# A decoder layer on one core: its first product taken on the raw input, its norm multiplied in afterwards, and the last product's end in smaller pieces

## The chip, the cores and the metric

The kernel runs on one core of a Trainium2 chip. The metric is device time in microseconds (us). Three timed runs of the kernel before gave 757.86, 758.69 and 758.94, so the median is 758.69 us. Engines are named as the profile names them: PE is TensorE (PEld its weight loads), DVE is VectorE, ACT is ScalarE, POOL is GpSimd, and SP issues most of the transfers.

## The reference

A decoder layer on 512 tokens of width 1024, in fp32.

```
h = rms_norm(x, g_mix);  proj = h @ w_in
q, k, v, qi, ki, wi, conv_in, qc, gate_pre = split_cols(proj, ...)
y_att  = top-k sparse attention: index scores from qi, ki, wi choose 256 keys a row
bg, cg, u = split(conv_in);  y_conv = (bg * causal_dwconv(cg * u)) @ w_conv_out
mem_kv = rms_norm(mem, g_mem) @ w_mem_kv;  y_mem = attention of qc on the memory @ w_mem_out
merged = gates0 * y_att + gates1 * y_conv + gates2 * y_mem;  x = x + merged @ w_o
h = rms_norm(x, g_ffn);  x = x + (silu(conv(gate)) * conv(val)) @ w_down
return rms_norm(x, g_final)
```

`rms_norm(a, g)` is `a * rsqrt(mean(a*a) + 1e-6) * g` over each row.

## The kernel before

Every large product is made of three matmuls: both factors are split into a high part `hi` (a rounded copy, made by ACT) and a low part `lo` (the rest, a subtraction on DVE), and hi·hi, lo·hi and hi·lo are added in one PSUM bank. A chunk of `w_in` (512 KB) comes over SP's queue into a `raw` buffer, is split, and meets the eight 128-row chunks of the normalised input `h` in 24 matmuls with 512 columns (L150 to L152 in the trace). Most of PE's time is that.

The head, in its order:
- The memory's key and value product: the transposed memory and its weights arrive as `mkv`, 48 matmuls of 512 columns into two PSUM banks (`pkv`).
- The norm of x: four row blocks are squared on ACT with a sum (L265), POOL takes the power -1/2, the four row factors are put on diagonals (`dg`, by DVE and ACT, L312 and L315), and two matmuls with ones spread them over all partitions as `rb` (L318).
- For each of the eight chunks of x transposed (`xn`, four tiles of two chunks with the gains and 424 columns of `w_in` beside them): DVE multiplies by gain and `rb` (L345), ACT makes hi (L348), DVE lo (L351). The 424 columns are keys, values and index projections by rows; their 12 matmuls a chunk are the rows product `pn` (L354, L356, L358), 96 in all.
- The first projections of the short convolution, by channels: `cg`, `u` and `bg`, 24 matmuls each, then the same for the second third, and so on. Between them the index queries and keys are copied by ACT to the places where the score matmuls want them (`Q`, L455, sixteen copies; `K`, L444) and their low parts are moved by DMA; the score matmuls are L463.

The order on each engine is written by a scheduler at build time, except that instructions inside `keep(...)` stay in the order of the program. Eight PSUM banks are in three pools: four "at", three "mm" and one "o" (L104). A new tile of a pool waits until the one whose bank it takes was read for the last time.

The tail is `w_down`: 22 chunks stream through with eight banks open (`stream_rows`), the last three are held, and each bank is finished in turn. `after_down` adds x, squares with a sum on ACT, multiplies by g_final, takes the power on POOL, and scales both halves of the row block before it is written.

Of the kernel before, what the change touches and what calls it, by code (L numbers as in the profile page):

```python
# [17 lines left out]
P = 128  # L18
# [75 lines left out]
def layer(ctx, tc, x, mem, g_ffn, g_final, w_in, x_n, m_kv, w_cm, w_att, w_o, w_up, w_down,  # L94
# [148 lines left out]

    kv_tags = ("oath", "oatl", "ocvh", "ocvl")
    mkv, rows = [], []
    for c in range(KD // 2):
        n = 1 if c == 0 else 2
        raw = op.tile([P, 2, M + 2 * CW + 1], F32, tag=kv_tags[c], name="mkv")
        for i in range(0, 2, n):
            keep(nc.sync.dma_start(raw[:, i:i + n], m_kv[2 * c + i:2 * c + i + n].rearrange("k p c -> p k c")))  # L250
        mkv.append(raw)
        if c == 2:
            rows += [first_rows(x, b, wp, "raw", 3) for b in range(2)]
    rows += [first_rows(x, 2, wp, "raw", 3), first_rows(x, 3, op, "omeh")]
    xn = []
    for c in range(KD // 2):
        raw = ea.tile([P, 2, S + NW + 1], F32, name=f"xn{c}")
        keep(nc.sync.dma_start(raw, x_n[2 * c:2 * c + 2].rearrange("k p c -> p k c")))
        xn.append(raw)
# [14 lines left out]
    ss = ea.tile([P, 2, NB], F32, name="ss")  # L274
    pkv = [bank("o"), bank()]
    for c, raw in enumerate(mkv):
        hi = wp.tile([P, 2, 2 * CW], F32R, tag="whi", name="whi", bufs=3)
        lo = wp.tile([P, 2, 2 * CW], F32R, tag="wlo", name="wlo", bufs=3)
        for ks in ([0], [1]) if c == 0 else ([0, 1],):
# [31 lines left out]
    dg = op.tile([P, 2, NB, P], F32R, tag="ocvh", name="dg")  # L311
# [4 lines left out]
    rb = bank()  # L316
    for i in range(2):
        keep(nc.tensor.matmul(rb, ones_r, dg[:, i].rearrange("p b s -> p (b s)"), start=i == 0, stop=i == 1))  # L318

    ready = {}  # L320

    def ahead(c0):

        src = w_in[IN_STARTS.index(c0)]
        raw = wp.tile(list(src.shape), F32, tag="raw", name="raw", bufs=3)
        keep(nc.sync.dma_start(raw, src))
        hi = wp.tile(list(src.shape), F32R, tag="whi", name="whi", bufs=3)
        lo = wp.tile(list(src.shape), F32R, tag="wlo", name="wlo", bufs=3)
        keep(nc.scalar.activation(hi, raw, AF.Copy))
        keep(nc.vector.tensor_sub(lo, raw, hi.bitcast(F32)))  # L330
        ready[c0] = hi, lo


    kr = op.tile([P, MB, CW], F32, tag="oath", name="kr")
    rm = ea.tile([P, MB], F32, name="rm")
    vms = [pkv[b][:, CW:].rearrange("p (h d) -> p h d", d=HD) for b in range(MB)]
    pn = [bank("at") for b in range(NB)]
    for c, raw in enumerate(xn):
        wh = ea.tile([P, 2, NW], F32R, name=f"wnh{c}")
        wl = ea.tile([P, 2, NW], F32R, name=f"wnl{c}")  # L340
        w = raw[:, :, S:S + NW]
        for j in range(2):
            k = 2 * c + j
            xt = raw[:, j, :S]
            keep(nc.vector.scalar_tensor_tensor(xt, xt, raw[:, j, S + NW:], rb, op0=ALU.mult, op1=ALU.mult))  # L345
            if j == 0:
                keep(nc.scalar.activation(wh, w, AF.Copy))
            keep(nc.scalar.activation(h[0][:, k], xt, AF.Copy))  # L348
            if j == 0:
                keep(nc.vector.tensor_sub(wl, w, wh.bitcast(F32)))  # L350
            keep(nc.vector.tensor_sub(h[1][:, k], xt, h[0][:, k].bitcast(F32)))  # L351
            bs = [slice(b * P, (b + 1) * P) for b in range(NB)]
            for b in range(NB):
                keep(nc.tensor.matmul(pn[b][:, :NW], h[0][:, k, bs[b]], wh[:, j], start=k == 0, stop=False))  # L354
            for b in range(NB):
# [29 lines left out]
    ahead(C_U)  # L385
    for t in range(3):
# [21 lines left out]
    nc.vector.tensor_scalar_mul(bgT, bgT, 0.5)  # L408
# [340 lines left out]
    def stream_rows(w, act, kc, tail, done, sp):  # L749
# [13 lines left out]
        last = [wrows(w, k, sp) for k in range(kc - tail, kc)]  # L763
# [8 lines left out]
    h2 = (h2p.tile([P, KD, S], F32R, name="h2h"), h2p.tile([P, KD, S], F32R, name="h2l"))  # L772
# [140 lines left out]
```

## Time and profile before

| | |
|---|---|
| median of three runs | 758.69 us |
| the profiled execution | 758.13 us |
| span of its trace | 756.3 us |
| PE busy | 739.1 us, 98% of the span |
| share of PE in the chain that ended last | 95% |

The span is what the trace covers; the execution's own time is 1.83 us longer. The chain of waits is followed back from the last instruction, so its shares say which engine the end hung on. In a timeline row come the start, the duration, the engine, the line, the operation with output and inputs, and in square brackets the idle time ahead of it and what ended that.

### The profile page before, as it was taken

The page shows a single profiled execution, that of the slowest core. Times are in us where ns is not written, and L with a number is a line of the kernel's source. Part 1 is how long each engine was busy: PE and PEld are TensorE (multiplying, and loading weights), DVE is VectorE, ACT ScalarE, POOL GpSimd, SP SyncE. Part 2 cuts the span into 40 slices and gives each one's busy share as a digit, 9 for nine tenths or more (in the row PEclk, how much of TensorE's full clock was granted, in tenths as well). Part 3 has the DMA queues.
Part 4 walks back from the last instruction along what each step waited for, and adds up shares of the span by engine and source line. Part 5 has one row for each costly group of instructions (what it writes and reads, how often), then busy time and mean ns, then how long its engine had stood idle before and what let it go on. Part 6 is the DMA issues. An engine that isn't in the chain of part 4 may idle for free.

```text
span 756.3 us, 9061 instructions
## 1 busy us (share of the span) xinstructions
PE 739.1 (98%) x3428; PEld 616.7 (82%) x3428; DVE 466.8 (62%) x787; ACT 341.2 (45%) x566; POOL 17.4 (2%) x42
## 2 busy tenths in 40 slices
PE   6899999999999999999999999999999999999995
PEld 4788888888888888888899888888888888888884
DVE  4756999999777763385466565656565654121215
ACT  6658465686455543244235434343434343121214
POOL 0100002000000000000010000000000000000001
PEclk9999999999999999999999999999999999999998
DMA  9725234522122224244403232322223232323202
GB/s 340 285 95 181 84 113 125 168 66 81 56 92 74 73 74 177 92 140 140 139 29 102 94 100 96 94 101 90 105 87 109 86 110 81 114 84 111 84 28 112
DMA packets 25931, 83.37 MB, mean 110 GB/s; under 512 B 3264, under 2 KB 4416, under 8 KB 25888
## 3 DMA queue, kind: packets, MB, share of 16 engines
q1 hardware_dynamic: 25744, 82.53, 32.6%
q8 instruction: 27, 0.44, 0.2%
q10 hardware_dynamic: 144, 0.26, 0.1%
q14 instruction: 16, 0.13, 0.1%
HBM read 77.34 MB, written 2.10 MB: 105 GB/s over the span
## 4 chain that ended last, share of the span: by engine, by line
PE 95%; DMA 1%; ACT 1%; DVE 1%; issue 0%; POOL 0%; SPq 0%; POOLq 0%; ACTq 0%
PE ps_mm L151 19%; PE ps_mm L150 19%; PE ps_mm L152 19%; PE ps_at L150 9%; PE ps_at L152 9%; PE ps_at L151 9%; DMA mkv<-m_kv 1%; PE ps_at L668 1%; PE ps_o L699 1%; PE ps_at L354 1%; PE ps_at L356 1%; PE ps_at L358 1%; PE ps_at L685 1%; PE ps_o L152 1%; PE ps_o L151 1%; PE ps_o L150 1%
## 5 line engine op out<-in xcount | busy, mean ns | idle before, releaser
L161 DVE TENSOR_TENSOR wlo<-raw,whi 128x1024 fp32r<-128x1024 f32 (+2 forms) x122 | 144.7, 1187 | 193.0 <-ACT whi L160 192.9
L160 ACT ACTIVATE whi<-raw 128x1024 fp32r<-128x1024 f32 (+2 forms) x122 | 125.8, 1032 | 181.2 <-PE ps_o L152 82.3
L150 PE MATMUL ps_mm<-hhi,whi 128*128 128x512 f32 x312 | 122.4, 392 | 0.0
L151 PE MATMUL ps_mm<-hlo,whi 128*128 128x512 f32 x312 | 122.1, 391 | 0.0
L152 PE MATMUL ps_mm<-hhi,wlo 128*128 128x512 f32 x312 | 122.1, 392 | 0.0
L151 PE MATMUL ps_at<-h2l,whi 128*128 128x512 f32 (+1 forms) x216 | 78.9, 366 | 0.0
L152 PE MATMUL ps_at<-h2h,wlo 128*128 128x512 f32 (+1 forms) x216 | 78.8, 365 | 0.0
L150 PE MATMUL ps_at<-h2h,whi 128*128 128x512 f32 (+1 forms) x216 | 78.7, 366 | 0.0
L151 PEld LDWEIGHTS ps_mm<-hlo,whi 128*128 128x128 f32 x312 | 58.6, 188 | 11.6
L152 PEld LDWEIGHTS ps_mm<-hhi,wlo 128*128 128x128 f32 x312 | 58.6, 188 | 11.6
L150 PEld LDWEIGHTS ps_mm<-hhi,whi 128*128 128x128 f32 x312 | 58.6, 188 | 11.5
L150 PE MATMUL ps_mm<-h2h,whi 128*128 128x512 f32 x160 | 62.2, 389 | 0.0
L151 PE MATMUL ps_mm<-h2l,whi 128*128 128x512 f32 x160 | 62.2, 389 | 0.0
L152 PE MATMUL ps_mm<-h2h,wlo 128*128 128x512 f32 x160 | 62.2, 389 | 0.0
L151 PEld LDWEIGHTS ps_at<-h2l,whi 128*128 128x128 f32 x216 | 40.7, 189 | 6.6
L152 PEld LDWEIGHTS ps_at<-h2h,wlo 128*128 128x128 f32 x216 | 40.7, 189 | 6.5
L150 PEld LDWEIGHTS ps_at<-h2h,whi 128*128 128x128 f32 x216 | 40.6, 189 | 6.5
L151 PEld LDWEIGHTS ps_mm<-h2l,whi 128*128 128x128 f32 x160 | 30.0, 188 | 6.3
L152 PEld LDWEIGHTS ps_mm<-h2h,wlo 128*128 128x128 f32 x160 | 30.0, 188 | 6.2
L150 PEld LDWEIGHTS ps_mm<-h2h,whi 128*128 128x128 f32 x160 | 30.0, 188 | 6.2
L832 ACT ACTIVATE t<-t 128x512 f32<-128x512 f32 x22 | 13.9, 633 | 44.8 <-DVE t L514 44.7
L160 ACT ACTIVATE acth<-t 128x512 fp32r<-128x512 f32 x14 | 8.8, 632 | 40.4 <-DVE t L833 40.4
(276 smaller groups left out, 1296.0 us busy)
## 6 DMA issues: line engine op xcount, KB each, us to landing
raw<-w_up SPq DMA_DIRECT2D x44, 512.0 KB, 3.5
raw<-w_in SPq DMA_DIRECT2D x39, 512.0 KB, 3.3
raw<-w_down SPq DMA_DIRECT2D x22, 512.0 KB, 3.4
raw<-w_o SPq DMA_DIRECT2D x8, 512.0 KB, 3.5
xn<-x_n SPq DMA_DIRECT2D x4, 937.0 KB, 13.9
raw<-w_cm SPq DMA_DIRECT2D x8, 320.0 KB, 2.9
mkv<-m_kv SPq DMA_DIRECT2D x3, 769.0 KB, 8.4
rows<-x SPq DMA_DIRECT2D x4, 512.0 KB, 10.8
```

The lines of the kernel that those rows point to most:

```text
L150: nc.tensor.matmul(o, sh, mh, start=first, stop=False)
L151: nc.tensor.matmul(o, sh, ml, start=False, stop=False)
L152: nc.tensor.matmul(o, sl, mh, start=False, stop=last)
L160: nc.scalar.activation(hi, src, AF.Copy)
L161: nc.vector.tensor_sub(lo, src, hi.bitcast(F32))
L354: keep(nc.tensor.matmul(pn[b][:, :NW], h[0][:, k, bs[b]], wh[:, j], start=k == 0, stop=False))
L356: keep(nc.tensor.matmul(pn[b][:, :NW], h[0][:, k, bs[b]], wl[:, j], start=False, stop=False))
L358: keep(nc.tensor.matmul(pn[b][:, :NW], h[1][:, k, bs[b]], wh[:, j], start=False, stop=k == KD - 1))
L668: nc.tensor.matmul(pb[:, :N], QS[:, hd, b * P:(b + 1) * P], KS[i][:, g, :N], start=(i == 0), stop=(i == 1))
L685: nc.tensor.transpose(pt[:, kb * P:(kb + 1) * P], lt[:, kb * P:(kb + 1) * P], ident)
L699: nc.tensor.matmul(po[:, q0:], V[:, kb, g, :], PT[i][:, c], start=(kb == 0 and i == 0), stop=(kb == NB - 1 and i == 1))
L832: nc.scalar.activation(tt[0], tt[0], AF.Silu)
```

## The change

The rows product no longer waits for the norm of x. It takes x times the gain, split into `xh` and `xl`; its result is multiplied by the row factor `rx` where it is read out of PSUM (`rn`, V and `wiN`). The first `cg` projection also runs on these raw parts (tile `pc`), and its result is multiplied by `rb` into `cg0`. The normalised `h`, which all other projections need, is made later in pieces (`h_split`) between these steps. `rb` is now copied from PSUM to SBUF by ACT. The transfers of the head are put in another order: the memory's weights first, then x's columns and rows mixed. The squares of the memory's rows, their power and the scaled copies out of `pkv` move behind the sixteen `Q` copies, so both banks of `pkv` stay taken until then. PE starts with 15 transposes of the identity whose results nobody reads.

In the tail the last product holds four chunks instead of three, in the buffers of `h2`; the last bank's 512 columns are finished as two pieces of 256, and the product with g_final goes to a tile of its own, ahead of the sum of squares.

The diff, cut to what the text speaks of:

```diff
+    idle = bank("at")
+    for i in range(15):
+        keep(nc.tensor.transpose(idle[:, :P], ident, ident))
...
-        n = 1 if c == 0 else 2
+        n = 1 if c < 2 else 2
...
+    first_cols(0, 0, 2)
+    rows += [first_rows(x, b, wp, "raw", 3) for b in range(3)]
+    first_cols(1, 0, 1)
+    rows.append(first_rows(x, 3, op, "omeh"))
+    first_cols(1, 1, 1)
+    first_cols(2, 0, 2)
+    first_cols(3, 0, 2)
+    ready = {}
+    def early(c0):
+        src = w_in[IN_STARTS.index(c0)]
+        raw = wp.tile(list(src.shape), F32, tag="raw", name="raw", bufs=3)
+        keep(nc.sync.dma_start(raw, src))
+        ready[c0] = raw
+    early(C_CG)
+    keep(nc.sync.dma_start(ropeN, rope_n))
+    early(C_U)
     memn = [first_rows(mem, 0, op, "omel"), first_rows(mem, 1, op, "omeh")]
-    keep(nc.sync.dma_start(ropeN, rope_n))
     keep(nc.sync.dma_start(par, params))
+    early(C_BG)
...
+    pn = [bank("at") for b in range(NB)]
+    xg = [op.tile([P, 3, S], F32R, tag=t, name="xg") for t in kv_tags] + [ea.tile([P, 2, S], F32R, name=f"xg{i}") for i in range(2)]
+    xh = [xg[k // 3 * 2][:, k % 3] for k in range(KD)]
+    xl = [xg[k // 3 * 2 + 1][:, k % 3] for k in range(KD)]
+    wn = []
...
+        keep(nc.scalar.activation(wh[:, sl], w, AF.Copy))
+        for j in js:
+            keep(nc.scalar.activation(xh[2 * c + j], raw[:, j, :S], AF.Copy, scale=raw[:, j, S + NW:]))
+        keep(nc.vector.tensor_sub(wl[:, sl], w, wh[:, sl].bitcast(F32)))
+        for j in js:
+            keep(nc.vector.scalar_tensor_tensor(xl[2 * c + j], raw[:, j, :S], raw[:, j, S + NW:], xh[2 * c + j].bitcast(F32),
+                                                op0=ALU.mult, op1=ALU.subtract))
...
+    def h_split(*ks):
+        for k in ks:
+            xt = xn[k // 2][:, k % 2, :S]
+            keep(nc.vector.scalar_tensor_tensor(xt, xt, xn[k // 2][:, k % 2, S + NW:], rb, op0=ALU.mult, op1=ALU.mult))
+            keep(nc.scalar.activation(h[0][:, k], xt, AF.Copy))
+            keep(nc.vector.tensor_sub(h[1][:, k], xt, h[0][:, k].bitcast(F32)))
...
+    cols_split(0, [0, 1])
+    rows_products(0, 1)
+    for b in range(3):
+        squares(rows[b], ss[:, 0, b:b + 1])
+    cols_split(1, [0])
+    rows_products(2)
+    squares(rows[3], ss[:, 0, 3:4])
     rx = ea.tile([P, NB], F32, name="rx")
     rh = ea.tile([P, NB], F32R, name="rh")
     rl = ea.tile([P, NB], F32, name="rl")
     power(ss[:, 0], rx)
+    cols_split(1, [1])
...
+    rb, cg0 = (lambda t: (t[:, 0], t[:, 1]))(g0p.tile([P, 2, S], F32, tag="g0", name="rb"))
+    cols_split(2, [0, 1])
+    keep(nc.scalar.activation(rb, pr, AF.Copy))
+    rows_products(4, 5)
+    h_split(0)
+    cols_split(3, [0, 1])
+    rows_products(6, 7)
+    h_split(1)
     ahead(C_CG)
-    for b in range(MB):
-        keep(nc.vector.scalar_tensor_tensor(VM[:, b, :, HD:], vms[b], rm[:, b:b + 1], VM[:, b, :, 0:HD].bitcast(F32),
-                                            op0=ALU.mult, op1=ALU.subtract))
-    rn = op.tile([P, NB, NIH + 1, IDXD], F32, tag="ocvl", name="rn")
+    h_split(2, 3, 4)
+    pc = bank()
+    for k in range(KD):
+        wh, wl = (x[:, k, :] for x in ready[C_CG])
+        for i, (a, b) in enumerate(((wh, xh[k]), (wh, xl[k]), (wl, xh[k]))):
+            keep(nc.tensor.matmul(pc, a, b, start=k == 0 and i == 0, stop=k == KD - 1 and i == 2))
...
     ahead(C_U)
+    h_split(5)
+    keep(nc.vector.tensor_mul(cg0, pc, rb))
+    h_split(6, 7)
+    ahead(C_BG)
...
+    rm = const.tile([P, MB], F32, name="rm")
+    for b in range(MB):
+        squares(memn[b], ss[:, 1, b:b + 1])
+    power(ss[:, 1, :MB], rm)
...
+        keep(nc.scalar.activation(kr[:, b], pkv[b][:, :CW], AF.Copy, scale=rm[:, b:b + 1]))
+        keep(nc.scalar.activation(VM[:, b, :, 0:HD], v, AF.Copy, scale=rm[:, b:b + 1]))
...
+        if c == 0:
+            cg = cg0
+        else:
+            pc = project(C_CG + c * P)
+            cg = rp.tile([P, S], F32, tag="rr", name="rr", bufs=2)
+            nc.scalar.activation(cg, pc, AF.Copy)
...
+                fin = fine and (b, hf) == (NB - 1, 1)
+                n = 256 if fin else 512
                 for i, wt in enumerate(last):
-                    step(b, kc - tail + i, wt, hf)
-                done(b, hf * 512, hf * 512 + 512, acc[b][hf])
+                    step(b, kc - tail + i, wt, hf, 0, n)
+                done(b, hf * 512, hf * 512 + n, acc[b][hf][:, :n])
+                if fin:
+                    rest = bank("at")[:, :n]
+                    for i, wt in enumerate(last):
+                        step(b, kc - tail + i, wt, hf, n, 512, rest, kc - tail)
+                    nc.vector.tensor_add(x1[:, b, D - n:], acc[b][hf][:, n:], x1[:, b, D - n:])
+                    done(b, D - n, D, rest)
...
+        xg = fp.tile([P, 512], F32, tag="t0", name="xg", bufs=2)
+        tc.keep_in_program_order(nc.vector.tensor_mul(xg, x1[:, b, 512:], gl[:, 512:]))
+        nc.vector.tensor_add(st[:, 0:1], st[:, 0:1], s1)
...
-    stream_rows(w_down, act, NF, 3, after_down, wp)
...
+    tails = [h2p.tile([P, 4, KD, P], F32R, tag=n, name="t" + n) for n in ("h2h", "h2l")]
+    def hold(i, src):
+        raw = load(src.rearrange("p (k c) -> p k c", c=P))
+        with tc.high_priority(offset=400):
+            split(tails[0][:, i], tails[1][:, i], raw)
+        return tails[0][:, i], tails[1][:, i]
+    stream_rows(w_down, act, NF, 4, after_down, hold, fine=True)
```

The scheduler's order around the second third of the convolution, on ACT. `Q` and `K` are the index copies, `rr` the copy of a finished `cg` out of PSUM, `rs` its first tap. Before:

```order
L520 ACTIVATE rr<-ps_mm 128x512
L396 ACTIVATE rQ<-ps_at 128x384 x2
L160 ACTIVATE hvh<-rQ 128x384
L455 ACTIVATE Q_478<-rQ 32x384 x3
L394 ACTIVATE rK<-ps_at 32x512
L329 ACTIVATE whi<-raw 128x1024
L160 ACTIVATE whi<-raw 128x1024
L455 ACTIVATE Q_478<-rQ 32x384 x8
L160 ACTIVATE hvh<-rQ 128x384
L455 ACTIVATE Q_478<-rQ 32x384 x2
L444 ACTIVATE K_479<-rK 32x512
```

The same engine and place now. Ahead of these rows, from the last high part of `h` on, stand two `whi`, two `rQ`, one `rK` and a third `whi`:

```order
L160 ACTIVATE hvh<-rQ 128x384
L504 ACTIVATE Q_538<-rQ 32x384 x11
L493 ACTIVATE K_539<-rK 32x512
L504 ACTIVATE Q_538<-rQ 32x384 x4
L160 ACTIVATE hvh<-rQ 128x384
L504 ACTIVATE Q_538<-rQ 32x384
L287 ACTIVATE rows,ss<-rows 128x1024
L160 ACTIVATE whi<-raw 128x1024
L287 ACTIVATE rows,ss<-rows 128x1024
L590 ACTIVATE rs<-rb,par 128x512
L160 ACTIVATE whi<-raw 128x1024
L585 ACTIVATE rr<-ps_mm 128x512
```

The copy `rr` of the first `cg` is gone; the two squares of the memory's rows (L287) have come behind the sixteen `Q` copies, and the copy `rr` of the second `cg` out of PSUM is last.

On PE, at the end of the second `cg` projection; `ps_mm_831` before and `ps_mm_876` now is the second `u` projection, and the matmuls from K4 and Q4 are the first index scores. Before:

```order
L152 MATMUL ps_mm_789<-hhi_84,wlo_793 128x512
L150 MATMUL ps_mm_831<-hhi_84,whi_834 128x512
L151 MATMUL ps_mm_831<-hlo_85,whi_834 128x512
L152 MATMUL ps_mm_831<-hhi_84,wlo_835 128x512
L150 MATMUL ps_mm_831<-hhi_84,whi_834 128x512
L151 MATMUL ps_mm_831<-hlo_85,whi_834 128x512
L152 MATMUL ps_mm_831<-hhi_84,wlo_835 128x512
L150 MATMUL ps_mm_831<-hhi_84,whi_834 128x512
L151 MATMUL ps_mm_831<-hlo_85,whi_834 128x512
L463 MATMUL ps_at_526<-K4_479,Q4_478 128x256
```

Now:

```order
L152 MATMUL ps_mm_834<-hhi_84,wlo_838 128x512
L525 MATMUL ps_at_598<-K4_539,Q4_538 128x256
L525 MATMUL ps_at_601<-K4_539,Q4_538 128x256
L525 MATMUL ps_at_606<-K4_539,Q4_538 128x256
L525 MATMUL ps_at_611<-K4_539,Q4_538 128x256
L525 MATMUL ps_at_616<-K4_539,Q4_538 128x256
L150 MATMUL ps_mm_876<-hhi_84,whi_879 128x512
```

Five score matmuls have come ahead of the second `u` projection, where eight of its matmuls stood ahead of the first score before.

On DVE, where `h` is made; `hlo` is its low part, `xg` the low part of x times the gain, `wnl` that of the 424 columns. Before:

```order
L345 SCALAR_TENSOR_TENSOR xn_138<-xn_138,ps_mm 128x512
L351 TENSOR_TENSOR hlo<-xn_138,hhi 128x512
L345 SCALAR_TENSOR_TENSOR xn_140<-xn_140,ps_mm 128x512
L350 TENSOR_TENSOR wnl_367<-xn_140,wnh_366 128x848
L351 TENSOR_TENSOR hlo<-xn_140,hhi 128x512
L345 SCALAR_TENSOR_TENSOR xn_140<-xn_140,ps_mm 128x512
L351 TENSOR_TENSOR hlo<-xn_140,hhi 128x512
L330 TENSOR_TENSOR wlo<-raw,whi 128x1024
```

Now:

```order
L340 TENSOR_TENSOR wnl<-xn_145,wnh 128x848
L342 SCALAR_TENSOR_TENSOR xg<-xn_145,xg 128x512 x2
L360 SCALAR_TENSOR_TENSOR xn_143<-xn_143,rb 128x512
L362 TENSOR_TENSOR hlo<-xn_143,hhi 128x512
L340 TENSOR_TENSOR wnl<-xn_146,wnh 128x848
L342 SCALAR_TENSOR_TENSOR xg_269<-xn_146,xg_268 128x512 x2
L360 SCALAR_TENSOR_TENSOR xn_143<-xn_143,rb 128x512
L362 TENSOR_TENSOR hlo<-xn_143,hhi 128x512
L369 TENSOR_TENSOR wlo<-raw,whi 128x1024
L360 SCALAR_TENSOR_TENSOR xn_144<-xn_144,rb 128x512
L362 TENSOR_TENSOR hlo<-xn_144,hhi 128x512
```

When the last tile's columns are split, DVE had made six chunks of `h` and begun the seventh before, and has made one now. The second follows at once, three more behind the low part of the `cg` weights, and the last three only behind the rope of the index rows (`rn`) and the low part of the `u` weights.

## Rows read from the trace of the kernel before

**Rows 1.** The page: the chain that ended last, by engine.

```profile
PE 95%; DMA 1%; ACT 1%; DVE 1%; issue 0%; POOL 0%; SPq 0%; POOLq 0%; ACTq 0%
```

**Rows 2.** PE's waits: total us, number of times, longest.

```profile
PE ps_o L295 <- ACT mT L285: 6.0, 3, 4.8
PE ps_at L354 <- ACT hhi L348: 1.5, 1, 1.5
```

**Rows 3.** Timeline of ACT around the norm of x.

```profile
15.10 1.06 ACT L282 ACTIVATE whi<-mkv 128x1024 fp32r<-128x1024 f32 x1 [0.62 <-DMA mkv<-m_kv]
...
18.86 0.19 ACT L265 ACTIVATION_READ_ACCUMULATOR rows<-rows 128x1 f32 x1
20.95 1.28 ACT L315 ACTIVATE dg<-ident,rl 128x128 fp32r<-128x128 f32 x4 [1.91 <-DVE rl L310]
```

**Rows 4.** Windows: us, busy of PE, PEld, DVE, ACT, POOL; PEclk, DMA share, GB/s.

```profile
23.00:24.00 1.00, 0.00 (x0) 0.00 (x0) 1.00 (x2) 0.43 (x2) 0.00 (x0) 1.00 1.04 416
24.00:25.00 1.00, 0.71 (x3) 0.69 (x4) 1.00 (x2) 0.23 (x1) 0.00 (x0) 0.84 1.02 409
25.00:26.00 1.00, 1.00 (x5) 0.93 (x4) 0.78 (x2) 0.18 (x1) 0.00 (x0) 0.50 1.04 418
```

**Rows 5.** Timeline of DVE: making h, then the rope stretch.

```profile
23.48 1.03 DVE L350 TENSOR_TENSOR wnl<-xn,wnh 128x848 fp32r<-128x848 f32 x1
24.43 0.69 DVE L351 TENSOR_TENSOR hlo<-xn,hhi 128x512 fp32r<-128x512 f32 x1
25.04 0.74 DVE L345 SCALAR_TENSOR_TENSOR xn<-xn,ps_mm 128x512 f32<-128x512 f32 x1
26.48 0.69 DVE L351 TENSOR_TENSOR hlo<-xn,hhi 128x512 fp32r<-128x512 f32 x1 [0.70 <-ACT hhi L348]
27.09 0.74 DVE L345 SCALAR_TENSOR_TENSOR xn<-xn,ps_mm 128x512 f32<-128x512 f32 x1
...
44.11 0.84 DVE L376 COPY rn<-ps_at 128x288 f32<-128x288 f32 x2 [1.22 <-PE ps_at L358]
...
47.55 1.22 DVE L330 TENSOR_TENSOR wlo<-raw,whi 128x1024 fp32r<-128x1024 f32 x1
```

**Rows 6.** ACT by line, 50 to 66 us: busy us, mean ns | idle before.

```profile
L455 ACT ACTIVATE Q<-rQ 32x384 fp32r<-32x384 f32 x16 | 8.4, 522 | 0.2
L160 ACT ACTIVATE whi<-raw 128x1024 fp32r<-128x1024 f32 x2 | 2.1, 1055 | 0.0
L160 ACT ACTIVATE hvh<-rQ 128x384 fp32r<-128x384 f32 x2 | 1.1, 526 | 0.0
L396 ACT ACTIVATE rQ<-ps_at 128x384 f32<-128x384 f32 x2 | 0.9, 488 | 0.1
L444 ACT ACTIVATE K<-rK 32x512 fp32r<-32x512 f32 x1 | 0.6, 632 | 0.0
```

**Rows 7.** DMA issues, 40 to 75 us: KB each, median us to landing.

```profile
Q<-hvl SPq DMA_DIRECT2D x16, 48.0 KB, 1.9
```

**Rows 8.** Timeline of PE: rows product, then first matmuls of projections.

```profile
24.29 1.45 PE L354 MATMUL ps_at<-wnh,hhi 128*128 128x424 f32 x4 [1.50 <-ACT hhi L348]
...
28.25 0.94 PE L354 MATMUL ps_at<-wnh,hhi 128*128 128x424 f32 x4
29.03 0.94 PE L356 MATMUL ps_at<-wnl,hhi 128*128 128x424 f32 x4
...
56.56 0.39 PE L150 MATMUL ps_mm<-hhi,whi 128*128 128x512 f32 x1
...
67.44 0.39 PE L150 MATMUL ps_mm<-hhi,whi 128*128 128x512 f32 x1
```

**Rows 9.** Timeline of the tail.

```profile
748.67 0.69 DVE L844 TENSOR_TENSOR x<-ps_o,x 128x512 f32<-128x512 f32 x1
749.39 0.63 ACT L845 ACTIVATE y<-x 128x512 f32<-128x512 f32 x1 [0.25 <-DVE x L844]
...
752.10 0.40 ACTq L859 DMA_DIRECT2D out<-y  x1
```

More of the change, by code (lines that the diff above doesn't have):

```diff
@@ L251, in layer, with first_cols @@
         mkv.append(raw)
[L252 to L259, printed above, removed]
+    xn = [ea.tile([P, 2, S + NW + 1], F32, name=f"xn{c}") for c in range(KD // 2)]
+    def first_cols(c, i, n):
+        keep(nc.sync.dma_start(xn[c][:, i:i + n], x_n[2 * c + i:2 * c + i + n].rearrange("k p c -> p k c")))
+    first_cols(0, 0, 2)
[14 more added lines that the diff above has]
+    early(C_U)
     memn = [first_rows(mem, 0, op, "omel"), first_rows(mem, 1, op, "omeh")]
-    keep(nc.sync.dma_start(ropeN, rope_n))
     keep(nc.sync.dma_start(par, params))
+    early(C_BG)
     def squares(src, dst):
@@ L278, in layer @@
         lo = wp.tile([P, 2, 2 * CW], F32R, tag="wlo", name="wlo", bufs=3)
-        for ks in ([0], [1]) if c == 0 else ([0, 1],):
+        for ks in ([0], [1]) if c < 2 else ([0, 1],):
             w = raw[:, ks[0]:ks[-1] + 1, M:M + 2 * CW]
@@ new lines, in layer, with cols_split @@
+    wn = []
+    def cols_split(c, js):
+        raw = xn[c]
+        if js[0] == 0:
+            wn.append([ea.tile([P, 2, NW], F32R, tag="wn" + i, name="wn" + i, bufs=2) for i in "hl"])
+        wh, wl = wn[c]
+        sl = slice(js[0], js[-1] + 1)
+        w = raw[:, sl, S:S + NW]
+        keep(nc.scalar.activation(wh[:, sl], w, AF.Copy))
[5 more added lines that the diff above has]
+                                                op0=ALU.mult, op1=ALU.subtract))
@@ new lines, in rows_product, with rows_products @@
+    def rows_product(k, part):
+        w = wn[k // 2][part == 1][:, k % 2]
+        for b in range(NB):
+            keep(nc.tensor.matmul(pn[b][:, :NW], (xl if part == 2 else xh)[k][:, b * P:(b + 1) * P], w,
+                                  start=k == 0 and part == 0, stop=k == KD - 1 and part == 2))
+    def rows_products(*ks):
+        for k in ks:
+            for part in range(3):
+                rows_product(k, part)
+    def h_split(*ks):
+        for k in ks:
+            xt = xn[k // 2][:, k % 2, :S]
+            keep(nc.vector.scalar_tensor_tensor(xt, xt, xn[k // 2][:, k % 2, S + NW:], rb, op0=ALU.mult, op1=ALU.mult))
+            keep(nc.scalar.activation(h[0][:, k], xt, AF.Copy))
+            keep(nc.vector.tensor_sub(h[1][:, k], xt, h[0][:, k].bitcast(F32)))
@@ new lines, in ahead @@
+    def ahead(c0):
+        raw = ready[c0]
+        hi = wp.tile(list(raw.shape), F32R, tag="whi", name="whi", bufs=3)
+        lo = wp.tile(list(raw.shape), F32R, tag="wlo", name="wlo", bufs=3)
+        keep(nc.scalar.activation(hi, raw, AF.Copy))
+        keep(nc.vector.tensor_sub(lo, raw, hi.bitcast(F32)))
+        ready[c0] = hi, lo
+    cols_split(0, [0, 1])
[4 more added lines that the diff above has]
+    rows_products(2)
@@ L315, in layer @@
         keep(nc.scalar.activation(dg[:, 1, b], ident, AF.Copy, scale=rl[:, b:b + 1]))
-    rb = bank()
+    rows_product(3, 0)
+    rows_product(3, 1)
+    pr = bank()
     for i in range(2):
[L318 to L331, printed above, removed]
@@ L456, in layer @@
                 move(Q4[64 + 32 * i:96 + 32 * i, 4 * t + j, :], ql[src])
+    rm = const.tile([P, MB], F32, name="rm")
+    for b in range(MB):
+        squares(memn[b], ss[:, 1, b:b + 1])
+    power(ss[:, 1, :MB], rm)
+    kr = op.tile([P, MB, CW], F32, tag="omel", name="kr")
+    for b in range(MB):
+        v = pkv[b][:, CW:].rearrange("p (h d) -> p h d", d=HD)
+        keep(nc.scalar.activation(kr[:, b], pkv[b][:, :CW], AF.Copy, scale=rm[:, b:b + 1]))
+        keep(nc.scalar.activation(VM[:, b, :, 0:HD], v, AF.Copy, scale=rm[:, b:b + 1]))
+        keep(nc.vector.scalar_tensor_tensor(VM[:, b, :, HD:], v, rm[:, b:b + 1], VM[:, b, :, 0:HD].bitcast(F32), op0=ALU.mult,
+                                            op1=ALU.subtract))
     for b in range(1, NB):
```

95 lines of the change are left out of this document (32 added, 63 removed).

## The prediction, written before the result was known

> **What bounds the kernel now.** I read the page first: the chain that ended last is 95% PE [rows 1]. So time is won only where PE waits, and any new wait of PE is paid in full. The list of PE's waits comes next: 4.8 us at the start for the memory's first operand, 1.5 us in one piece for the first `hi` of h [rows 2], and little else. Then the windows and the timeline of the stretch around that wait: PE idles for the whole of 23 to 24 us, and for most of 24 to 26 us the granted clock is half, 0.84 and then 0.50 [rows 4]. The twelve matmuls of the first chunk of the rows product start at 24.29 and the next chunk at 28.25, 3.96 us, where later four take 29.03 - 28.25 = 0.78, so twelve 2.34 [rows 8]. The wait thus costs about 1.6 us again in clock behind it. The change goes for this place. After it PE runs without a wait: the first `bg` projection starts at 56.56 and the second `u` projection at 67.44, two projections or 48 matmuls later, 10.88 / 48 = 0.2267 us each [rows 8].
>
> **The start.** The 15 transposes stand in PE's first wait of 4.8 us [rows 2], so I put them at nothing. Were they longer than that wait they would cost up to 1 us, but they would still end ahead of the place that decides below.
>
> **The factor `rb` comes later.** The four row blocks of x are now mixed with the columns. Ahead of the end of the fourth, SP's queue has moved 6.69 MB (by the tiles' shapes, mkv 3.15, `xn0` 0.96, half of `xn1` 0.48, four row blocks 2.10); before, 4.20 MB (mkv 3.15 and two row blocks) had landed when ACT took the last mkv at 15.10 [rows 3]. At 411 GB/s, the middle of 409 to 418 [rows 4], the 2.49 MB more are 6.06 us: the last block lands at 21.2, and its square, priced as the `whi` of the same 1024 columns at 1.1 [rows 3], ends at 22.3. From the end of the squares (18.86 + 0.19 = 19.05) to the end of `dg` (20.95 + 1.28 = 22.23) it took 3.18 [rows 3]; so `dg` ends at 25.5 on ACT, against 22.2. The rows product does not wait for it, which is the gain. But `h` does, and all projections but one need `h`.
>
> **DVE then makes `h` in a queue.** A chunk takes 27.09 - 25.04 = 2.05: multiply, 0.70 of waiting for ACT's hi, subtract [rows 5]. The split of x adds work that was not there: a tile's two `xg`, priced as the multiply at 0.70 each, beside the `wnl` of 24.43 - 23.48 = 0.95 [rows 5]. Behind `dg`, ACT makes the next tile's hi (1.0). Then DVE does two blocks of `wnl`, two `xg` and one chunk, 4.4 each; the low part of the `cg` weights 1.15; three chunks 6.15; `rn` and rope, as 47.55 - 44.11 = 3.44; the low part of the `u` weights 1.15; one chunk 2.05; `cg0` 0.7; two chunks 4.1. [rows 5] That is 27.5, from 26.5 to 54.0. The last chunk's hi is 0.61 earlier (its subtract), at 53.4. With two or three matmuls behind, the first `u` ends at 54.7, 1.9 ahead of before. PE has waits in this stretch, but they lie beside DVE's queue. The low part of the `bg` weights, behind that last hi, is ready only at 53.4 + 1.0 + 1.15 = 55.6, which takes some 0.8 back: the head gains about 1.1, and the second `cg` ends at about 66.4.
>
> **ACT then has everything at once.** This is the step that decides. Before, the index copies `Q` were spread from 52 us on. Now all of them stand behind the last hi of `h`, and ahead of `rr`, which frees the PSUM bank of the second `cg`. Because `pkv` keeps its "mm" bank until after the index copies, only two such banks go round, and the second `u` projection must have the one that `rr` frees. From 53.4 ACT has: five `whi` 5.25, two `rQ` 0.9, two `hvh` 1.1, sixteen `Q` 8.4, one `K` 0.6 [rows 6]; one `rK`, the tap `rs` and `rr`, each priced as that `K` of 512 columns, 1.9; and two squares, priced as `whi`, 2.1. That is 20.2. Long instructions back to back overlap by about 0.08, as 23.48 + 1.03 against 24.43 on DVE [rows 5]; for twelve or so that is 1.0 less. So `rr` ends at 53.4 + 19.2 = 72.6, and the second `u` starts there against 67.44: 5.2 late. The five first scores are done by then; 256 columns at 0.78 / 4 x 256 / 424 = 0.12 each [rows 8] give back 0.6. The lag is 4.6. The low ends: if fewer of these instructions stand in the way, it falls to the wait for the moves (a rival below); the high end, with every instruction at its full mean and the last hi at 54.0, is 6.2.
>
> **The clock.** Between 66.4 and 72.6 PE would have five short matmuls. In the trace before, PE had two from 20 us to 24.29, and the clock fell to 0.50 for 1.6 us' worth of loss. I take 1.6 again; the bounds are 0 and twice that, 3.3, if two such stretches follow. The Trainium skill ("TensorE: Matmul & The Clock Gate", section "HAM oscillation — how this bites in real kernels") says that a wait between bursts of matmuls makes the next burst start at the low clock, and that each such wait pays anew. The fall after 23 us in this trace agrees; by the rule the sum has the 1.6, without it 0.
>
> **The tail.** From the last add at 748.67 to the output's transfer at 752.10 are 3.43 us [rows 9]. A last piece of 256 columns makes the add (0.69) and the square (0.63) shorter, by 0 to a half; I take 0.35 together. The product with g_final hides beside the square. The 24 short matmuls in place of 12 cost 24 x 0.12 - 12 x 0.2267 = 0.15. Net -0.2, between -0.7 and +0.2. The fourth held chunk moves work that PE does anyway: nothing.
>
> **Sum.** Against the profiled 758.13: lag 4.6 + clock 1.6 - tail 0.2 = +6.0, so 764.1; the median was 0.56 above the profiled run, so 764.7. The head's gain of 1.1 does not appear in it: it is swallowed by the wait for ACT.
>
> **Rivals.**
> - The clock stays up during the second wait, as five score matmuls lie in it and the waits are in several pieces. For it: they are more than the two `dg` matmuls of 20 to 24 us. Against it: the whole is longer. Then 764.7 - 1.6 = 763.1.
> - The bank is not what holds the second `u`; only the index copies and their moves do. The sixteenth `Q` ends about 4.5 ahead of `rr` (two squares, two `whi`, `rs` and `rr`, less overlap), at 67.9; its low part needs 1.9 from issue to landing [rows 7], so the last scores end at about 70.2. Lag 70.2 - 67.44 - 0.6 = 2.2: 760.7 with the clock up, 762.3 with it down. Against it: the order of PE and `rr`'s place at the very end of ACT's list.
> - Worse: DVE's queue is longer (ACT, which serves it with hi, also has V, `rn` and the weights between), so that the last hi comes at 55, or the clock falls for two stretches. 1.6 more: 766.3, up to 768.
> - Not slower: ACT keeps up and PE never waits there, as before, when ACT had the same copies and PE had none of its waits in this stretch. PE then starts the second `u` at 67.0 with the scores done, 1.04 better, and the tail gives 0.2: 757.4. It decides if `rr` ends by 67 us, 5.6 earlier than I work out; sixteen `Q` alone take 8.4 behind a chunk that cannot come before `rb`. Its ends are 756.5 and 758.7.
>
> **How the numbers follow.** The forecast 0.50, the clock stays 0.19, only the index copies 0.10, worse 0.09, not slower 0.12. This measurement tells 0.2%, 1.5 us, from no change. Half of the last case is below 757.2 and half within the bound: faster 0.06, same 0.07 (with a little from the index copies), slower 0.87. The range goes from 760.0 to 768.0: it holds the first four cases and the bounds of the lag and of the clock, and leaves out the last one.
>
> **What would show it.** In the trace after: `dg` ends near 25.5; the rows product has no wait for hi of h; the last `hlo` ends near 54; ACT is without a gap from 53 to 73; PE has a wait for the scores from 66 and then one of some 2 us for the second `u` that ends with ACT's `rr`; the granted clock falls behind it. The tail from the last add to the output's transfer is about 0.3 shorter. Wrong would be a `rr` that ends before 68, a third free bank, or a fourth row block that lands before 19 us, which would bring all later steps forward by as much.

## The result: 0.9% slower, and the profile after

The changed kernel takes 765.49 us in the median of three runs against 758.43 (ratio 1.0093, 95% interval 1.0073 to 1.0113), 7.1 us more. Forecast were 764.7 us and a range of 760.0 to 768.0. A fourth run, the profiled one, was disturbed as a whole (2792 us) and is left out of this median, and all rows here are from a second trace of the same kernel, whose four runs gave 765.72 us in the median (ratio 1.0093, interval 1.0079 to 1.0107). Its span is 764.0 us, 7.7 above that of before.

The chain that ended last, by engine, answers to [rows 1]; PE's share has fallen from 95% to 89%:

```profile
PE 89%; ACT 2%; DVE 1%; issue 1%; POOLq 0%; POOL 0%; ACTq 0%
```

PE's longer waits, in total us, number and longest, answer to [rows 2]. The wait for the first hi of h is gone, and so are most of the 6.0 us for the memory's operands, where the transposes now stand: the memory's first matmul starts at 4.82 as against 4.78. Later in the head others have come:

```profile
PE ps_at L439 <- DVE rn L427: 2.4, 1, 2.4
PE ps_mm L150 <- ACT rr L585: 2.0, 1, 2.0
PE ps_mm L150 <- ACT whi L368: 1.7, 1, 1.7
...
PE ps_at L525 <- DMA K<-kl: 1.4, 1, 1.4
PE ps_at L525 <- DMA Q<-hvl: 1.4, 2, 0.9
```

The second row and the last two, four waits, are one stretch in the timeline of PE. The last matmul of the second `cg` starts at 67.15; the five scores come in three pieces, each after a wait for a transfer; the second `u` starts at 73.95, when ACT's `rr` has freed its bank, where [rows 8] have 67.44:

```profile
67.15 0.39 PE L152 MATMUL ps_mm<-hhi,wlo 128*128 128x512 f32 x1
68.97 0.60 PE L525 MATMUL ps_at<-K,Q 128*128 128x256 f32 x3 [1.43 <-DMA K<-kl]
70.06 0.36 PE L525 MATMUL ps_at<-K,Q 128*128 128x256 f32 x1 [0.48 <-DMA Q<-hvl]
71.36 0.55 PE L525 MATMUL ps_at<-K,Q 128*128 128x256 f32 x1 [0.94 <-DMA Q<-hvl]
73.95 0.79 PE L150 MATMUL ps_mm<-hhi,whi 128*128 128x512 f32 x1 [2.04 <-ACT rr L585]
...
77.53 0.52 PE L152 MATMUL ps_mm<-hhi,wlo 128*128 128x512 f32 x1
77.89 0.39 PE L150 MATMUL ps_mm<-hhi,whi 128*128 128x512 f32 x1
```

The chain that ended last passes through `rr` into this `u`, and not through the transfers:

```profile
73.42 0.49 ACT rr L585
...
73.95 0.79 PE ps_mm L150
```

The nine matmuls from 73.95 to 77.89 take 3.94 us, at 0.2267 each they would take 2.04: 1.9 lost. The windows of this stretch and of the earlier one around the rope (columns as in [rows 4]) show why. The granted clock is at half from about 47 us, when the wait for the rope ends, to 50.5, and again from 71, while PE still waits, until 77.8.

```profile
48.00:50.00 2.00, 2.00 (x10) 1.75 (x10) 1.30 (x3) 0.63 (x1) 0.00 (x0) 0.50 0.26 49
...
71.00:72.00 1.00, 0.55 (x1) 0.29 (x1) 1.00 (x1) 1.00 (x3) 0.06 (x1) 0.50 0.38 88
...
76.00:77.00 1.00, 1.00 (x4) 0.80 (x3) 1.00 (x4) 0.97 (x3) 0.00 (x0) 0.50 0.95 344
77.00:78.00 1.00, 1.00 (x4) 0.77 (x4) 1.00 (x3) 0.00 (x0) 0.00 (x0) 0.60 0.84 221
```

The timeline of ACT: from the last hi of h at 53.92 to the end of `rr` at 73.89 it has no gap. The index copies begin at 58.94. Three `whi` stand ahead of them; behind them stand the two squares of the memory's rows, two more `whi` and the tap `rs`. The first row is the diagonals `dg`, which end at 24.61 + 1.28 = 25.89.

```profile
24.61 1.28 ACT L391 ACTIVATE dg<-ident,rl 128x128 fp32r<-128x128 f32 x4 [1.16 <-DVE rl L386]
...
53.92 0.63 ACT L361 ACTIVATE hhi<-xn 128x512 fp32r<-128x512 f32 x1 [1.43 <-DVE xn L360]
54.46 1.04 ACT L368 ACTIVATE whi<-raw 128x1024 fp32r<-128x1024 f32 x1
...
58.94 5.86 ACT L504 ACTIVATE Q<-rQ 32x384 fp32r<-32x384 f32 x11
...
68.72 1.06 ACT L287 ACTIVATE rows<-rows 128x1024 f32<-128x1024 f32 x1
...
73.32 0.57 ACT L585 ACTIVATE rr<-ps_mm 128x512 f32<-128x512 f32 x1
```

And the timeline of DVE, whose queue for h begins at 26.73 behind `dg` and ends with the last low part at 55.28:

```profile
26.73 1.04 DVE L340 TENSOR_TENSOR wnl<-xn,wnh 128x848 fp32r<-128x848 f32 x1 [1.61 <-ACT wnh L337]
...
43.24 0.94 DVE L419 TENSOR_SCALAR rn<-ps_at,rx 128x288 f32<-128x288 f32 x2
...
47.30 1.22 DVE L369 TENSOR_TENSOR wlo<-raw,whi 128x1024 fp32r<-128x1024 f32 x1
...
54.59 0.69 DVE L362 TENSOR_TENSOR hlo<-xn,hhi 128x512 fp32r<-128x512 f32 x1 [0.70 <-ACT hhi L361]
```

PE reaches the last low part of `h` before DVE has it, and begins the first `bg` at 55.90:

```profile
55.33 0.50 PE L151 MATMUL ps_mm<-hlo,whi 128*128 128x512 f32 x1 [0.23 <-DVE hlo L362]
...
55.90 0.40 PE L150 MATMUL ps_mm<-hhi,whi 128*128 128x512 f32 x1
```

### The profile page after: what moved, and what is told of

It reads as the page before. It is cut to its first block, busy times and chain, and to the rows that moved or that the text cites. A ratio compares the mean times of both kernels' runs of the same rounds, so it can differ in the third digit from the quotient of the medians.

```text
span 2790.2 us, 9151 instructions
## 1 busy us (share of the span) xinstructions
PE 2781.8 (100%) x3455; PEld 1585.2 (57%) x3455; DVE 480.9 (17%) x801; ACT 351.9 (13%) x578; POOL 16.9 (1%) x42
## 4 chain that ended last, share of the span: by engine, by line
PE 99%; issue 1%; DVE 0%; POOL 0%; ACT 0%; POOLq 0%
PE ps_mm L152 19%; PE ps_mm L150 19%; PE ps_mm L151 19%; PE ps_at L152 9%; PE ps_at L151 9%; PE ps_at L150 9%; PE ps_at L348 4%; PE ps_mm L413 1%; PE ps_o L764 1%; PE ps_at L733 1%; PE ps_at L750 1%; PE ps_o L152 1%; PE ps_o L150 1%; PE ps_o L151 1%; PE ps_at L525 1%
## 5 line engine op out<-in xcount | busy, mean ns | idle before, releaser
L150 PE MATMUL ps_mm<-hhi,whi 128*128 128x512 f32 x304 | 355.8, 1170 | 0.0
L152 PE MATMUL ps_mm<-hhi,wlo 128*128 128x512 f32 x304 | 354.8, 1167 | 0.0
L151 PE MATMUL ps_mm<-hlo,whi 128*128 128x512 f32 x304 | 354.3, 1166 | 0.0
L151 PE MATMUL ps_at<-h2l,whi 128*128 128x512 f32 (+1 forms) x216 | 217.9, 1009 | 0.0
L152 PE MATMUL ps_at<-h2h,wlo 128*128 128x512 f32 (+1 forms) x216 | 217.7, 1008 | 0.0
L150 PE MATMUL ps_at<-h2h,whi 128*128 128x512 f32 (+1 forms) x216 | 217.4, 1008 | 0.0
L152 PEld LDWEIGHTS ps_mm<-hhi,wlo 128*128 128x128 f32 x304 | 147.2, 484 | 113.3 <-issue 112.3
L152 PE MATMUL ps_mm<-h2h,wlo 128*128 128x512 f32 x160 | 176.0, 1100 | 0.0
L150 PE MATMUL ps_mm<-h2h,whi 128*128 128x512 f32 x160 | 175.9, 1099 | 0.0
L151 PE MATMUL ps_mm<-h2l,whi 128*128 128x512 f32 x160 | 175.9, 1099 | 0.0
```

The lines of the kernel that those rows point to most:

```text
L150: nc.tensor.matmul(o, sh, mh, start=first, stop=False)
L151: nc.tensor.matmul(o, sh, ml, start=False, stop=False)
L152: nc.tensor.matmul(o, sl, mh, start=False, stop=last)
```

## The experiments

Theory A is the prediction's: the second `u` waits for the bank that `rr` frees, `rr` stands at the end of ACT's long queue, and the clock falls behind the wait. The rivals: B, only the index copies and their moves hold PE; C, the head itself is late; D, part of the loss is the tail's. Every edit is against the changed kernel unless said otherwise, and every ratio is to the kernel before on the same chip: 758.43 us for the first four runs, 759.03 for "Work from the start of the wait" and "And work for PE during the rope", 758.52 for the other four. Differences from the changed kernel are from its 765.72 us.

**The same kernel again.** No edit.

> The changed kernel once more, unaltered, for a trace. Theory A (the second u projection waits for the PSUM bank that ACT's copy rr frees at the end of a long queue): 764 to 767 us; PE waits from about 66 to 72.6 us in pieces, the last of them ended by ACT's rr copy (L585), and the granted clock falls behind it. Rival B (only the index copies and their moves hold PE): the long wait ends with the first scores (L525), and the second u projection starts without a wait behind them. Rival C (the head itself is late, by the order of the transfers and DVE's queue): the first u projection ends later than 56.6 us.

Measured: 765.72 us. The rows above are its trace. The last wait ends with `rr`, as A has it. The three waits that B names are there too, 2.85 us in all, but the last of them ends 2 us ahead of `rr`. C is wrong by its own sign: the first `u` ends at 55.90, which is 0.66 ahead of before.

**The memory's squares early.**

```diff
-    h_split(2, 3, 4)
+    h_split(2)
...
+    squares(memn[0], ss[:, 1, 0:1])
+    h_split(3)
+    squares(memn[1], ss[:, 1, 1:2])
+    power(ss[:, 1, :MB], rm)
+    h_split(4)
...
     h_split(5)
+    kr = op.tile([P, MB, CW], F32, tag="omel", name="kr")
+    for b in range(MB):
...
+        keep(nc.scalar.activation(kr[:, b], pkv[b][:, :CW], AF.Copy, scale=rm[:, b:b + 1]))
+        keep(nc.scalar.activation(VM[:, b, :, 0:HD], v, AF.Copy, scale=rm[:, b:b + 1]))
...
```

What is added here has gone from behind the `Q` copies.

> The squares of the memory's rows, their power and the scaled copies out of pkv stand between the h pieces again, so that pkv's bank is free for the second u projection and ACT's queue has 2 us less behind the index copies. A: the wait of about 6 us and the slow clock behind it go, 757.5 to 760 us. B: the index copies and moves stay where they are, so most of the wait stays, 762 to 764. C: no gain, 765 or more, since these instructions lengthen the queue that makes h.

Measured: 758.86 us, ratio 1.0003 (0.9994 to 1.0012). Nearly the whole loss hangs on where six instructions of ACT stand (two squares and four copies; POOL's power and two instructions of DVE moved with them). In the windows of its trace PE is full from 66 to 70 us, at full clock:

```profile
66.00:67.00 1.00, 1.00 (x6) 0.82 (x5) 0.66 (x1) 0.96 (x3) 0.00 (x0) 1.00 0.34 77
67.00:70.00 3.00, 3.00 (x15) 2.48 (x14) 0.58 (x2) 2.90 (x6) 0.00 (x0) 1.00 0.36 82
```

A is right and C wrong as the main cause. B falls too, though this run does not part it from A cleanly: with a bank free the scheduler put the second `u` ahead of the first scores on PE, so their transfers are no longer waited for. Nor does it part the bank from the shorter queue, since it alters both; the next run does.

**The bank freed by DVE.**

```diff
-            nc.scalar.activation(cg, pc, AF.Copy)
+            if c == 1:
+                nc.vector.tensor_copy(cg, pc)
+            else:
+                nc.scalar.activation(cg, pc, AF.Copy)
```

> Only one thing is altered: the second cg is copied out of PSUM by DVE instead of ACT, so its bank is freed without ACT's queue. A: the wait ahead of the second u projection goes, that for the first scores (some 2 us) stays, 760 to 762.5 us. B: no change, 764 to 767. C: no change.

Measured: 760.36 us, ratio 1.0021 (1.0012 to 1.003), 5.4 below the changed kernel. ACT's queue is as long as before, less one copy, and PE's timeline shows which wait stayed: the one for the moved keys, 1.43 us. The clock does not fall behind it.

```profile
67.09 0.39 PE L152 MATMUL ps_mm<-hhi,wlo 128*128 128x512 f32 x1
68.91 0.61 PE L525 MATMUL ps_at<-K,Q 128*128 128x256 f32 x3 [1.43 <-DMA K<-kl]
69.35 0.46 PE L150 MATMUL ps_mm<-hhi,whi 128*128 128x512 f32 x1
```

So the copy's place costs 5.4 us of the loss, its clock included. Of what is left, 1.9 us against the kernel before, 1.43 is the wait for the moved keys. The two waits for moved queries are gone as well, because PE now has matmuls of `u` to do meanwhile.

**The tail alone**, on the head of before (the functions `stream_rows`, `after_down` and `hold` of the change).

> The head of the kernel before with the tail of the change (four held chunks, last 512 columns in two pieces, g_final beside the sum). A: 758.2 us, 0.2 less than before, between -0.7 and +0.2. Rival D (part of the loss is the tail's: 24 short matmuls, one more bank, the held chunks' splits): 759.5 or more.

Measured: 758.04 us, ratio 0.9991 (0.9982 to 1.0): 0.4 less, D is wrong. In its timeline the last add and the output's transfer are 2.63 us apart where [rows 9] have 3.43. POOL's power between them takes 0.55:

```profile
749.74 0.42 DVE L855 TENSOR_TENSOR x<-ps_at,x 128x256 f32<-128x256 f32 x1 [0.28 <-PE ps_at L152]
...
751.04 0.55 POOL L867 TENSOR_TENSOR st<-st,mhalf 128x1 f32<-128x1 f32 x1 [4.63 <-DVE st L866]
...
752.37 0.40 ACTq L873 DMA_DIRECT2D out<-y  x1
```

In the kernel before, the same power takes 0.92, with DVE's product with g_final beside it:

```profile
750.23 0.68 DVE L852 TENSOR_TENSOR x<-x,gl 128x512 f32<-128x512 f32 x1
750.39 0.92 POOL L853 TENSOR_TENSOR st<-st,mhalf 128x1 f32<-128x1 f32 x1 [2.61 <-DVE st L849]
```

**Work in the second part of the wait.**

```diff
         squares(memn[b], ss[:, 1, b:b + 1])
+        idle = bank("at")
+        for i in range((16, 8)[b]):
+            nc.tensor.transpose(idle[:, i % 4 * P:i % 4 * P + P], memn[b][:, i % 8 * P:i % 8 * P + P], ident)
```

> The changed kernel with 24 transposes of the memory's squared rows, whose results nobody reads, ahead of the first scores: 16 run when ACT has made the first square (about 70 us), 8 after the second (about 72), so PE is no longer idle for most of the wait. The second u projection still waits for rr. If the loss behind the wait is the clock (theory A's second term), the granted clock stays at full speed there and the time falls by 1.5 to 1.9 us, to 763.8 to 764.3. If the slow matmuls behind the wait have another cause, or the transposes don't hold the clock up, no change: 765 to 766.5.

Measured: 765.08 us, ratio 1.0086 (1.0072 to 1.01): no change that can be told from the changed kernel's 1.0093. That is outside what was expected if the clock is the cause (763.8 to 764.3), so by its time alone it speaks against the clock; the trace says why it does not. Before the first transpose PE was idle for 2.38 us. The clock was still full when it began, fell a us later and was back at the end of the transposes; the transposes themselves ran at half clock and, with the scores behind them, took so long that the second `u` came 1.71 us later than in the changed kernel, and then ran at full speed:

```profile
70.00:71.00 1.00, 0.77 (x7) 0.78 (x8) 0.00 (x0) 1.00 (x3) 0.00 (x0) 1.00 0.32 75
71.00:72.00 1.00, 1.00 (x7) 1.00 (x6) 0.84 (x1) 1.00 (x3) 0.00 (x0) 0.51 0.31 72
...
75.00:76.00 1.00, 0.78 (x5) 0.52 (x5) 1.00 (x3) 1.00 (x4) 0.00 (x0) 1.00 0.70 176
```

```profile
70.23 4.51 PE L513 MATMUL ps_at<-ident,rows 128*128 128x128 f32 x24 [2.38 <-ACT rows L287]
...
75.66 0.40 PE L150 MATMUL ps_mm<-hhi,whi 128*128 128x512 f32 x1
```

**Work from the start of the wait.**

```diff
-        ql = halves(r, ip, SQ)[1]
+        qh, ql = halves(r, ip, SQ)
+        if t == 1:
+            idle = bank("at")
+            for i in range(10):
+                nc.tensor.matmul(idle[:, :SQ], qh[:, :P], qh, start=True, stop=True)
...
         squares(memn[b], ss[:, 1, b:b + 1])
+        idle = bank("at")
+        for i in range(8):
+            nc.tensor.transpose(idle[:, i % 4 * P:i % 4 * P + P], memn[b][:, i * P:(i + 1) * P], ident)
```

> The wait of the changed kernel filled from nearly its beginning: ten matmuls of 384 columns on the second half of the index queries (ready at about 68.2 us), then eight transposes behind each of the two squares; nobody reads their results. The second u projection still waits for rr at about 73.5 to 74. If the clock falls because PE stood idle, it now stays at full speed through the wait, and the time falls by 1.5 to 1.9 us against the changed kernel, to 763.8 to 764.4. If these fillers don't count as work for the clock, or if the fall has another cause, the matmuls behind rr are slow again: 765 to 766.5.

Measured: 763.61 us, ratio 1.0065 (1.0052 to 1.0077), some 2.1 below the changed kernel. PE is at work again 0.66 us after the second `cg`, the windows keep the full clock, and the second `u` starts at 73.56, behind `rr` as ever, and at full speed: its first nine matmuls end at 75.73, after 2.17 us instead of 3.94:

```profile
67.81 2.03 PE L504 MATMUL ps_at<-hvh 128*128 128x384 f32 x10 [0.66 <-ACT hvh L160]
...
73.56 0.50 PE L150 MATMUL ps_mm<-hhi,whi 128*128 128x512 f32 x1
...
75.73 0.39 PE L150 MATMUL ps_mm<-hhi,whi 128*128 128x512 f32 x1
```

```profile
71.00:72.00 1.00, 0.49 (x4) 0.49 (x5) 0.68 (x1) 1.00 (x4) 0.37 (x2) 1.00 0.25 58
...
74.00:75.00 1.00, 1.00 (x6) 0.83 (x5) 1.00 (x2) 1.00 (x4) 0.00 (x0) 1.00 0.60 159
```

So the clock's part is shown: the wait alone costs what it lasts, and idling through it costs some 1.8 us more (3.94 - 2.17; the rest of the 2.1 is that the second `u` started 0.39 earlier here).

**h in an overlapped order on DVE.**

```diff
-            keep(nc.vector.tensor_sub(h[1][:, k], xt, h[0][:, k].bitcast(F32)))
...
+            if i:
+                low(ks[i - 1])
+        low(ks[-1])
...
-    h_split(5)
     keep(nc.vector.tensor_mul(cg0, pc, rb))
-    h_split(6, 7)
+    h_split(5, 6, 7)
```

(`low(k)` is the subtraction of chunk k; it now stands behind the multiplication of the next chunk. The multiplication that makes `cg0` stands ahead of the last three chunks, where it parted the first of them from the other two.)

> The changed kernel with one edit: DVE multiplies the next chunk of h before it subtracts the one before, so it does not wait 0.70 us for ACT's hi in most of the chunks. Theory A with the queue of DVE ahead of it: h is done some 3.5 us earlier, ACT's queue starts earlier by as much and rr with it: 761 to 763 us. If ACT's queue is set by something other than the last piece of h: no change, 765 to 766.5.

Measured: 762.23 us, ratio 1.0045 (1.0032 to 1.0057), 3.5 below the changed kernel. The timelines of ACT and PE show the last hi at 49.87 and the end of `rr` at 69.84, both 4.05 earlier, with the same 19.3 us between them; PE's wait has only moved:

```profile
49.87 0.63 ACT L364 ACTIVATE hhi<-xn 128x512 fp32r<-128x512 f32 x1 [0.76 <-DVE xn L363]
...
69.27 0.57 ACT L589 ACTIVATE rr<-ps_mm 128x512 f32<-128x512 f32 x1
```

```profile
66.28 0.71 PE L529 MATMUL ps_at<-K,Q 128*128 128x256 f32 x4 [1.92 <-DMA K<-kl]
...
69.90 0.80 PE L150 MATMUL ps_mm<-hhi,whi 128*128 128x512 f32 x1 [2.24 <-ACT rr L589]
```

That shows the first link of the chain: here the last hi came 4.05 us earlier, and so did the second `u`. Of the 4.05, 3.5 reach the median.

**Both edits.** The overlapped order, the memory's squares behind the fourth chunk of h, and the copies out of `pkv` straight behind the last:

```diff
+    h_split(2, 3)
...
+    squares(memn[0], ss[:, 1, 0:1])
+    squares(memn[1], ss[:, 1, 1:2])
+    power(ss[:, 1, :MB], rm)
+    h_split(4)
...
     h_split(5, 6, 7)
     ahead(C_BG)
+    kr = op.tile([P, MB, CW], F32, tag="omel", name="kr")
...
```

> Both edits together: h in the overlapped order, the memory's squares between its pieces, and the scaled copies out of pkv straight behind the last piece, so that a bank is free and no long wait is left. A: the two gains add, since one shortens what stands ahead of the index copies and the other takes the wait behind them: 754.5 to 756.5 us, faster than the kernel before. If the head is bound by something other than DVE's queue (the transfers, PE itself): 758 to 759, as with the early squares alone.

Measured: 756.46 us, ratio 0.9973 (0.9962 to 0.9984). The two gains, 3.5 and 6.9 by themselves, are 9.3 together, so they nearly add; that is the slow end of what A expected. PE's waits and a window show what is left, the wait for the rope and the slow clock behind it:

```profile
PE ps_at L455 <- DVE rn L437: 2.4, 1, 2.4
```

```profile
48.00:50.00 2.00, 2.00 (x7) 1.61 (x6) 1.96 (x4) 1.04 (x2) 0.00 (x0) 0.50 0.66 217
```

**And work for PE during the rope**, on top of both edits:

```diff
+    ahead(C_U)
     rn = ea.tile([P, NB, NIH + 1, IDXD], F32, name="rn")
...
     keep(nc.vector.tensor_add(a2, a2, rt[:, 1]))
-    ahead(C_U)
```

> As the version with both edits, and the split of the first u weights stands ahead of the rope instead of behind it, so that PE has some 13 matmuls of the first u projection to do while the rope is made, and is not idle for 2.4 us there. DVE has the same work in all, so the last piece of h comes no earlier. If the slow clock behind that wait (0.50 from 47 to 51 us) was on the path: 1 to 2 us less, 754.5 to 755.5. If h alone bounds this stretch: no change, 756 to 757.

Measured: 754.57 us, ratio 0.9946 (0.9932 to 0.9959), some 4 us faster than the kernel before and 1.9 below the version with both edits. The wait for the rope is 0.7 instead of 2.4. PE still has waits in these windows, but they lie between matmuls, and the clock stays full:

```profile
46.00:48.00 2.00, 1.57 (x7) 0.95 (x6) 2.00 (x10) 0.00 (x0) 0.00 (x0) 1.00 0.96 361
48.00:50.00 2.00, 1.28 (x10) 1.00 (x10) 2.00 (x4) 0.62 (x1) 0.00 (x0) 1.00 0.19 72
```

How much of the 1.9 is the clock is not shown: the edit also takes 13 matmuls of `u` out of the stretch behind the rope, and PE then waits for pieces of h instead.

**Without the 15 transposes at the start.**

```diff
-    idle = bank("at")
-    for i in range(15):
-        keep(nc.tensor.transpose(idle[:, :P], ident, ident))
```

> The changed kernel without the 15 transposes at its start. They stand in PE's first wait, and the head is set by DVE and ACT, so no change: 765 to 766.5 us. Rival: they keep the clock up for the memory's product, and without them the head is later by 1 us or more, 766.8 or above.

Measured: 765.99 us, ratio 1.0097 (1.0084 to 1.0111): no change from the changed kernel's 1.0093. PE's first wait is 5.1 us there, and nothing of it shows in the median.

## Why the prediction was right, and where its sizes were off

The mechanism was the one forecast, and two runs that take it away by different edits (the early squares and the copy on DVE) remove 6.9 and 5.4 us of the loss.

- **`rb` later:** forecast was the last row block at 21.2 and `dg`'s end at 25.5. The block landed at 21.1 (issued at 8.49, 12.6 to landing), `dg` ended at 25.89, and DVE's queue began at 26.73 against 26.5. Right within 0.4. The bandwidth used, 411, is not the middle of 409 to 418, which is 413.5; it moves the landing by 0.04.
- **DVE's queue for h:** forecast 27.5 us, measured 55.28 - 26.73 = 28.55. The mis-sized term is the rope stretch: 3.44 was taken over from before, where V and the weights of the index heads needed no factor; with the factor, and with one scaling and one of these weights more in it, it takes 47.30 - 43.24 = 4.06. Most of the rest is in the two blocks of `wnl`, two `xg` and a chunk, which took 4.53 and 4.68 and not 4.4 each. So the first `u` ended at 55.90 instead of 54.7, and the gain of the head, 1.1 by the forecast, was nearly nil: the last matmul of the second `cg` began at 67.15, so the `cg` ended at 67.38 where before it was 67.44. The sum did not count on that gain.
- **ACT's queue:** forecast 19.2 us from the last hi, measured 73.89 - 54.55 = 19.3. The last hi came 1.15 later than forecast, for DVE's sake, so `rr` ended at 73.9 instead of 72.6. The lag of the second `u` is 73.95 - 67.44 - 0.6 = 5.9 instead of 4.6. This term was the one most mis-sized, by 1.3.
- **The clock:** forecast 1.6, measured 1.9 in the trace, and 1.8 by the run that fills the wait. The rule of the Trainium skill that the prediction weighed ("TensorE: Matmul & The Clock Gate", section "HAM oscillation — how this bites in real kernels") held here: each of the two long waits, at 43 to 47 and at 67 to 74 us, each with a few matmuls in it, was followed by matmuls at 0.50 of the clock. The wait of 1.43 us in the run with the copy on DVE was not. What it costs depends on the path. The first one cost little or nothing in the changed kernel, by its rows: PE had caught up with DVE's queue at 55.33, where it waits for the last low part. In the version with both edits it was, together with the wait ahead of it, worth about 1.9 us (756.46 against 754.57).
- **The tail:** forecast -0.2, measured -0.4 with an interval from -1.4 to 0. From the last add to the transfer 0.8 went, not 0.35. From the add to the end of the square's sum 0.4 of it went (add and square of 256 columns took 0.42 each); the other 0.4 is POOL's power, 0.55 instead of 0.92, a term that the prediction did not have.
- **The sum:** in the traces 5.9 + 1.9 in the head, -0.8 + 0.15 in the tail, and 0.4 that was not forecast. From 377.89 to 389.09 us, in the product with `w_o`, 48 matmuls take 11.20 us at full clock and without a wait, where before (369.96 to 380.84) they took 10.88: a step of 0.2333 instead of 0.2267, and it goes on a little beyond. The run with the tail alone does not have it, all others with the new head do; its cause is open. That makes 7.55, against 7.7 between the traces and 7.1 between the medians. The forecast time came within 0.8 us of the median with a sum, 6.0, that is 1.5 too small; that it came so near is in part luck, since the traced runs of the two kernels lie further apart than their medians.
- **The rival with the index copies alone:** its three waits are there, 2.85 us, but they lie ahead of the wait for `rr` and cost nothing by themselves; without `rr` 1.43 of them was left. Its arithmetic has a slip: 4.5 ahead of 72.6 is 68.1 and not 67.9. The sixteenth `Q` in fact ended at 68.18 + 0.52 = 68.70, 5.2 ahead of the end of `rr`.

## What to carry to other kernels

Work that is taken off the critical engine's path comes back as a queue on the engines that serve it, and what decides is the last instruction in that queue that someone waits for: look for a PSUM copy at its end, and count the banks that are left to go round. Here six instructions of ACT in another place were worth 6.9 us. A multiply, copy and subtract chain over two engines was 3.5 us faster here when it was emitted one step apart. And a long wait of the matmul engine cost the clock as well: work put into it from its start took that back, work put in later did not.

## What the runs showed of the hardware

Work without a use, put into a wait to keep the clock up, helped in one run and not in the other. Where it began after 0.66 us of idle time the granted clock stayed at 1.00. Where it began after 2.38 us it fell to 0.51 although 24 transposes then ran without a gap, and was back at 1.00 before the useful matmuls began; the half speed had gone into the transposes, and the time stayed the same. The two runs also differ in the kind of work (ten matmuls of 384 columns stood ahead of the transposes in the first), so that the start alone makes the difference is not shown.

POOL's power on 128 numbers took 0.54 to 0.55 us in all four row blocks of the run with the tail alone, where DVE's product with g_final was done before it. In the kernel before it took 0.92 to 0.98 in the three blocks where a DVE multiplication out of SBUF stood beside it, and 0.54 in the one where DVE was adding out of PSUM.
